# Lags of a chunk's inner products: read from a lagged copy, or as offsets in the inputs on chip

## The chip, the cores and the metric

The kernel runs on one core of a Trainium2 chip. A core has a matrix engine (TensorE, PE in the profile; PEld is its weight load), a vector engine (VectorE, DVE), a scalar engine (ScalarE, ACT), GpSimd (POOL) and SyncE (SP), which here only issues transfers. Each engine works through its own queue in order; they meet at semaphores. Matrix products are written to PSUM, everything else lies in SBUF or in HBM. The metric is the time of one execution on the device, in microseconds; a kernel's time is the median of its runs.

## The reference

One inference step of a two-layer encoder for two groups of requests that share the weights: 256 new frames of one stream and 32 further frames of another, 288 positions with 2048 channels in all. Layer 0 is attention (two kinds of heads) with one input and one output projection. Layer 1, which the change touches, is a diagonal complex state-space layer: channels in groups of 16, each with 64 complex states.

```python
u, z = jnp.split(h @ p['w_in_ssm'][isd], 2, axis=-1)
...
bu_re = jnp.einsum('btgc,gpc->btgp', u, bb_re)
bu_im = jnp.einsum('btgc,gpc->btgp', u, bb_im)
...
ac_re, ac_im, x_re, x_im = lax.associative_scan(combine, (a_re, a_im, bu_re, bu_im), axis=1)
...
y = jnp.einsum('btgp,gcp->btgc', x_re, c_re) - jnp.einsum('btgp,gcp->btgc', x_im, c_im)
...
y = y.reshape(B, T, D_SSM) + p['ssm_d'][isd] * u32
g = jax.nn.gelu(y)
glu = g * jax.nn.sigmoid(g @ p['w_glu'][isd] + p['b_glu'][isd])
out = (glu.astype(x.dtype) * jax.nn.silu(z)) @ p['w_out_ssm'][isd]
```

## The kernel before

All weights stream in once, in tiles of 128 x 2048 (w, 1 MB, rows of 8192 bytes), through four staging slots. Each weight tile is split into a high and a low part (hi by ACT, lo by DVE), the activations likewise (ah, al), and each product is three matmuls into one accumulator m: hi x ah, hi x al, lo x ah. This main stream is some 6900 matmuls of 288 or 290 columns on PE.

The work around it, called side work, is a set of Python generators. A planner (`Plan`) keeps a clock for every engine from cost formulas, and `Tasks.step` lets a generator go on when its inputs are due by that clock. So the order of the instructions on each engine is fixed when the program is built, by planned costs; on the chip each queue then runs in that order, whatever is late. A change of a planned cost shifts the side work of its whole stage.

Layer 1 cuts the sequence into blocks of LC = 8 positions, NJ = 36 blocks in all, and stores positions so that index s (place in the block) is the slow one and j (block) the fast one: a row of 288 elements is 8 pieces of 36. The 2048 channels are 16 tiles of 128 (called chunks here, loop variable i, four of them a quarter). For each chunk:

- `builder` (during layer 0) makes three small matrices from the parameters and stores them in HBM: w1 for the state inputs, v2 for the outputs, and kb, which holds for each lag k the 16 x 16 products inside a block. kb comes from the accumulator k_ps.
- `state_in` stores a quarter of the layer's inputs U (in the buffer MX) to HBM (ud), loads it back regrouped into MX[:, 16:20], and multiplies with w1 (accumulator xin_ps) into X.
- `scan` carries the state from block to block on DVE, 32 steps for a quarter.
- `slices` multiplies the states with v2 (y_ps), evicts to Yg and stores to HBM (yd); `gelus` loads it back (yx) and finishes the layer's activation.
- `inside` adds the part of the output that comes from earlier positions of the same block: position s takes kb of lag k times the input at position s - k. In the row of 288, lag k is a shift by 36 k. The accumulator is t_ps; a DVE multiply-add then writes t_ps + D x U over U.

For `inside`, `lags` prepares a copy. ud has rows padded by 108 zeros; UL[n] is loaded from it with four transfers of 32 partitions, each with another lag l = 0 to 3, so that the 128 partitions of UL hold 4 lags x 32 channels, for each of the four groups of 32 channels. Then t_ps needs two matmuls of 128 rows for each group g of 32 output channels: a = 0 for lags 0 to 3 and a = 1 for lags 4 to 7, shifted by 144 columns. There are two UL buffers; one of them is a staging slot of the weights, taken from the moment when layer 1 starts (`taken`) until its states are done.

In the attention layer the lines of cached keys (CK) and values (CV) share one buffer, so a load of CK waits for the product that reads the CV before it (pvs_ps); Ss are the scores against CK.

Of the kernel before, what the change touches and what calls it, by code (L numbers as in the profile page):

```python
# [8 lines left out]
F32 = mybir.dt.float32  # L9
# [14 lines left out]
LC = 8  # L24
# [247 lines left out]
def build(tc, I, O):  # L272
# [8 lines left out]
    with ExitStack() as ctx:  # L281
# [103 lines left out]
        jobs = []  # L385
        st_of = {}
        pos = dict(load=0, run=0)
        st_free, slot_of, taken = list(range(NST)), {}, []
        more = dict(tiles={}, until=0)

        def pump():
# [16 lines left out]

        def st_done(k):
            del st_of[k]  # L410
            if taken and taken[0] is None:
                taken[0] = slot_of[k]
            else:
                st_free.append(slot_of[k])

        quarters = {}
        split = dict(live=0)
# [401 lines left out]
        def builder():  # L819
            bl_load(0)  # L820
            for i in range(KT):
                bl_load(i + 1)
                pt, raw = bl_in.pop(i)
                bb, rc = (raw[:, j].rearrange("p (g r c) -> p g r c", g=4, r=2) for j in range(2))
                plan.last = max(plan.when(plan.written, t) for t in (pt, raw))
                yield "dve"
                V = views(pt)
                bbar(V, bb)
                yield "next dve"
                v2 = bld.tile([128, 2, 4, 9, 16], F32, name="v2")  # L830
                for ri in range(2):
                    tsum(V, v2[:, ri, :, 0:8], bb, 8, *((("apr", 0), ("api", 1), ALU.subtract),
                                                        (("apr", 1), ("api", 0), ALU.add))[ri])
                    if ri == 0:
                        at = plan.last
                        yield "next dve"
                plan.last = at
                for ri in range(2):
                    yield "any"
                    yield from room()  # L840
                    ps = take([128, 4, 128], "w1_ps")
                    for g in range(4):
                        pe.transpose(ps[:, g, :], v2[:, ri, g, 0:8].rearrange("p k c -> p (k c)"), ident)
                    yield "act"
                    W1 = bld.tile([128, 4, 128], F32, tag="W%d" % ri, name="W1")
                    act.copy(W1, ps)
                    act.dma_start(w1_d[i, :, ri], W1)
                    give(ps)
                    plan.last = plan.when(plan.written, v2)
                yield "next dve"  # L850
                for ri in range(2):
                    tsum(V, v2[:, ri], rc, 9, *((("apr", 0), ("api", 1), ALU.subtract),
                                                (("api", 0), ("apr", 1), None))[ri])
                    if ri == 0:
                        yield "next act dve"
                        bp = bld.tile([128, 4, 2, 2, 16], F32, tag="W0", name="bp")
                        for e in range(2):
                            act.activation(bp[:, :, :, e, :], bb, AF.Copy, scale=hmask[:, e:e + 1])
                act.dma_start(v2_d[i], v2.rearrange("p r g k c -> p r (g k c)"))
                plan.last = plan.when(plan.written, v2)  # L860
                yield "any"
                yield from room()
                kps = take([128, 4, 2, 16], "k_ps")
                for g in range(4):
                    for ri in range(2):
                        for l in range(4):
                            mm(kps[32 * l:32 * l + 32, g], bp[:, g, ri].rearrange("p e c -> p (e c)"),
                               v2[:, ri, g, 3 - l:8 - l:4], start=ri == 0, stop=ri == 1)
                yield "act"
                kb = bld.tile([128, 4, 2, 2, 16], F32, tag="W1", name="kb")  # L870
                for e in range(2):
                    act.activation(kb[:, :, :, e, :], kps, AF.Copy, scale=kmask[:, e:e + 1])
                give(kps)
                act.dma_start(kb_d[i], kb.rearrange("p g a e c -> p (g a e c)"))
                plan.last = plan.done(v2.tensor.name)


# [599 lines left out]
        tsc(hbglu, hbglu, 0.5)  # L1477
        sfin = sp1.tile([128, 2, 64, 2], F32, name="sfin")
        sp.dma_start(sfin[:, 1], I["state"])
        PAD = 3 * NJ  # L1480
        ud = dram.tile([KT, 128, PAD + T], F32, name="ud")
        yd = dram.tile([KT, 128, T], F32, name="yd")
        x1d = dram.tile([128, KT, T], F32, name="x1d")
        U = MX
# [102 lines left out]
                act.dma_start(b, w1_d[k])  # L1587
                w1r.append(b)

        UL, ul_free = {}, []  # L1590

        def lags():

            zero = SZ[:, 0:6, :].rearrange("p a t -> p (a t)")
            pool.memset(zero, 0.0)
            sp.dma_start(ud[:, :, 0:PAD].rearrange("n p t -> p n t"), zero.rearrange("p (n t) -> p n t", n=KT))
            while taken[0] is None:
                yield "w any"
            t = wst.tile([128, 2048], F32, tag="w%d" % taken[0], name="UL")
            ul_free.extend((t[:, 0:4 * T], sl.tile([128, 4 * T], F32, name="UL1")))  # L1600
            row = PAD + T
            for n in range(KT):
                while ("ur", n // 4) not in ready or not ul_free:
                    yield "w any"
                UL[n] = ul_free.pop(0).rearrange("p (g t) -> p g t", g=4)
                for l in range(4):
                    sp.dma_start(UL[n][32 * l:32 * l + 32], bass.AP(ud.tensor, ud.offset + 128 * n * row + l * NJ,
                                                                    [[row, 32], [32 * row, 4], [1, T]]))
                ready.add(("ul", n))
                yield "next any"  # L1610

        def state_in():

            while taken[0] is None:
                yield "w"
            w1_ahead(0)
            for i in range(KT):
                if i % 4 == 0:
                    yield from wait(("u", i // 4))
                    sp.dma_start(ud[i:i + 4, :, PAD:].rearrange("n p t -> p n t"), U[:, i:i + 4, :])  # L1620
                    yield "act"
                    ready.add(("ur", i // 4))
                    ug = MX[:, 16:20, :].rearrange("p a (g j) -> p (a g) j", j=NJ)
                    src = ud[i:i + 4, :, PAD:].rearrange("n (g c) (s j) -> s c (n g) j", c=16, s=LC)
                    for s in range(LC):
                        sp.dma_start(ug[16 * s:16 * s + 16], src[7 - s])
                    yield "act"
# [59 lines left out]

        def kb_load(i):
            if i < KT:
                kbs[i] = sl.tile([128, 4, 2, 32], F32, tag="kb%d" % (i % 3), name="kb")  # L1690
                sp.dma_start(kbs[i].rearrange("p g a e -> p (g a e)"), kb_d[i])

        def slices():

# [33 lines left out]
        def inside():  # L1728

            for i in range(3):  # L1730
                kb_load(i)
            for i in range(KT):
                yield from wait(("ul", i))
                kb = kbs.pop(i)
                plan.last = max(plan.when(plan.written, UL[i]), plan.when(plan.written, kb))
                yield "dve"
                yield from room()
                tps = take([128, T], "t_ps")
                for a in range(2):
                    for g in range(4):  # L1740
                        mm(tps[32 * g:32 * g + 32, 4 * a * NJ:T], kb[:, g, a], UL[i][:, g, 0:T - 4 * a * NJ],
                           start=a == 0, stop=a == 1)
                ul_free.append(UL.pop(i).rearrange("p g t -> p (g t)"))
                kb_load(i + 3)
                dve.scalar_tensor_tensor(U[:, i, :], U[:, i, :], dT[:, i:i + 1], tps, op0=ALU.mult, op1=ALU.add)
                give(tps)
                ready.add(("yt", i))
                yield "next dve"
# [92 lines left out]
        early.close()  # L1841
        banks["mod"] = 0.0
        mod_sb[0] = lambda: sl.tile([128, 8, 8, 16], F32, tag="kb", name="modsb").rearrange("p a b c -> p (a b c)")
        taken.append(None)
        sl = tpool(pd, "sl", 1)
        side.add(state_in())
        side.add(lags())
        side.add(slices())
        side.add(inside())
        for ln in range(2):  # L1850
# [2 lines left out]
        run_jobs(l1b, 4)  # L1853
        side.until(lambda: "mod" in banks and ("yt", KT - 1) in ready)
        del banks["mod"]
        st_free.extend((taken[0], NST))
        free = X.rearrange("p a r j -> p (a r j)")
        more.update(tiles={NST: lambda: free[:, 0:2048].rearrange("p (k n) -> p k n", k=4)}, until=len(jobs))
        side.add(act_split("m1", "g", lambda c: [("glu", c)], lambda c: SZ[:, 4 * c:4 * c + 4, :]))
# [157 lines left out]
```

## Time and profile before

| what | value |
| --- | --- |
| median of 3 runs | 1380.06 us |
| runs | 1374.49, 1380.06, 1509.9 us |
| profiled execution | 1372.13 us |
| its span, first to last instruction | 1369.6 us |
| mean granted TensorE clock | 0.96 |
| moved by DMA | 344.90 MB in 125442 packets, mean 252 GB/s |
| UL loads | 64 transfers of 144 KB |
| store of zeros to ud | one transfer of 864 KB |

Every instruction is recorded through a helper at line 116, so groups are told apart by names: `t_ps<-UL,kb` is what writes t_ps and reads UL and kb. "128*32 128x288" is a matmul with 128 rows and 32 columns of weights that streams 288 columns. A matmul in f32 has two records. A row's last figures are the engine's idle time just before the group and what ended it. In a table by stage, clock and DMA share are means over the stretch. The weights' stream of layer 1 begins near 783 us; its input projection ends near 1122 us, and what follows is the GLU and the output projection.

### The profile page before, as it was taken

To read this page: it belongs to the slowest core of one execution; us is meant where nothing else is said; L and a number is where in the kernel's file an instruction comes from. 1 tells how busy PE (TensorE), PEld (TensorE's weight loads), DVE (VectorE), ACT (ScalarE), POOL (GpSimd) and SP (SyncE) were. 2 spreads that over 40 slices of the span, in tenths; PEclk is the share of its full clock that TensorE was granted. 3 is DMA by queue.
4 is the path that set the end of the run, shared out by engine and by line. 5 is a ranking of instruction groups with operands and counts; after the bars stand their busy time and mean duration, and the time that the engine had idled before them with its cause. 6 is when DMAs were issued, how large, how long until landed. Compare 5 with 4: busy or idle time off the path is not lost.

```text
span 1369.6 us, 28062 instructions
## 1 busy us (share of the span) xinstructions
PE 1237.1 (90%) x11098; PEld 1098.7 (80%) x11098; DVE 922.6 (67%) x2210; ACT 593.4 (43%) x1394; POOL 32.6 (2%) x21
## 2 busy tenths in 40 slices
PE   5999899999898999998899997875997998999996
PEld 3788798888787878886789896764986998989895
DVE  4579978788777877884556953745944965455454
ACT  4533233343454454454443743321553484444341
POOL 0006000000000000000000000000000000000000
PEclk9999999999999999999899998987988999999998
DMA  9978676688878878878665697989499366777631
GB/s 360 372 299 321 233 283 252 232 289 327 308 277 292 314 270 305 308 251 337 231 251 182 210 298 201 236 218 222 150 186 254 132 200 243 262 263 264 245 124 70
DMA packets 125442, 344.90 MB, mean 252 GB/s; under 512 B 50784, under 2 KB 75376, under 8 KB 94592
## 3 DMA queue, kind: packets, MB, share of 16 engines
q1 hardware_dynamic: 112640, 313.47, 67.9%
q10 hardware_dynamic: 12672, 29.65, 5.9%
q8 instruction: 87, 1.43, 0.4%
q14 instruction: 43, 0.35, 0.1%
HBM read 307.13 MB, written 35.95 MB: 250 GB/s over the span
## 4 chain that ended last, share of the span: by engine, by line
issue 44%; PE 32%; DVE 11%; DMA 10%; ACT 2%; POOL 0%; ACTq 0%; SPq 0%; DVEq 0%; POOLq 0%
PE m L116 24%; PE mod_ps L116 4%; DMA w<-in_w_in_att 4%; DVE lo L116 2%; DMA w_d<-W 2%; DMA v_d<-v 2%; DVE v L116 2%; DVE MX L116 1%; DVE tmpv L116 1%; ACT hi L116 1%; PE w_ps L116 1%; DVE qkv L116 1%; DVE dtmp L116 1%; DMA Fb<-Fp_d 1%; DVE ssq L116 1%
## 5 line engine op out<-in xcount | busy, mean ns | idle before, releaser
L116 PE MATMUL m<-ah,hi 128*128 128x288 f32 (+1 forms) x2304 | 714.6, 310 | 13.3 <-ACT hi L116 4.8
L116 PE MATMUL m<-ah,lo 128*128 128x288 f32 (+1 forms) x2304 | 689.8, 299 | 4.3 <-DVE lo L116 4.3
L116 PE MATMUL m<-al,hi 128*128 128x288 f32 (+1 forms) x2304 | 690.7, 300 | 0.4 <-DVE al L116 0.4
L116 PEld LDWEIGHTS m<-ah,hi 128*128 128x128 f32 x2304 | 443.0, 192 | 69.7 <-issue 32.3
L116 DVE TENSOR_TENSOR lo<-w,hi 128x512 fp32r<-128x512 f32 x552 | 368.4, 686 | 169.0 <-ACT hi L116 164.5
L116 ACT CAST hi<-w 128x512 fp32r<-128x512 f32 x552 | 322.0, 617 | 325.0 <-PE m L116 203.3
L116 PEld LDWEIGHTS m<-ah,lo 128*128 128x128 f32 x2304 | 443.2, 192 | 6.2 <-DVE lo L116 6.1
L116 PEld LDWEIGHTS m<-al,hi 128*128 128x128 f32 x2304 | 443.6, 193 | 1.0 <-DVE al L116 0.8
L116 PE MATMUL mod_ps<-w,cs 128*32 128x512 f32 x744 | 97.6, 619 | 12.6 <-DVE ssq L116 12.6
L116 DVE SCALAR_TENSOR_TENSOR qkv<-m,qkv 128x288 f32<-128x288 f32 x168 | 73.0, 452 | 25.9 <-PE m L116 25.7
L116 DVE TENSOR_TENSOR X<-X,t 128x32 f32<-128x32 f32 (+1 forms) x256 | 58.3, 228 | 8.2
L116 DVE TENSOR_TENSOR v<-pt,raw 128x512 f32<-128x512 f32 (+1 forms) x64 | 46.0, 718 | 13.5 <-DMA v_d<-v 13.4
L116 DVE SCALAR_TENSOR_TENSOR MX<-MX,c_dT,t_ps 128x288 f32<-128x288 f32 x16 | 8.2, 512 | 68.5 <-PE t_ps L116 68.5
L116 PE MATMUL t_ps<-UL,kb 128*32 128x288 f32 (+1 forms) x256 | 18.8, 420 | 38.4 <-DMA UL<-ud 38.4
L116 DVE SCALAR_TENSOR_TENSOR MX<-m,gate,MX 128x256 f32<-128x256 f32 x96 | 30.8, 363 | 32.2 <-PE m L116 32.1
L116 PEld LDWEIGHTS mod_ps<-w,cs 128*32 128x32 f32 x744 | 17.2, 110 | 38.0 <-issue 22.2
L116 DVE TENSOR_TENSOR tmpv<-pt,raw 128x512 f32<-128x512 f32 (+1 forms) x64 | 45.9, 718 | 0.0
L116 PEld LDWEIGHTS t_ps<-UL,kb 128*32 128x32 f32 x256 | 8.4, 124 | 46.1 <-issue 42.7
L116 PE MATMUL y_ps<-Xm,v 128*128 128x74 f32 x256 | 34.7, 294 | 10.4 <-DMA v<-v_d 5.3
L116 PEld LDWEIGHTS y_ps<-Xm,v 128*128 128x128 f32 x256 | 33.4, 210 | 11.4 <-ACT Xm L116 6.0
L116 ACT ACTIVATE yx<-MX 128x288 f32<-128x288 f32 (+1 forms) x38 | 18.8, 495 | 50.7 <-DVE MX L116 50.2
L116 DVE TENSOR_TENSOR v<-v,tmpv 128x512 f32<-128x512 f32 (+1 forms) x48 | 34.3, 714 | 1.7
(226 smaller groups left out, 910.6 us busy)
## 6 DMA issues: line engine op xcount, KB each, us to landing
w<-in_w_mod SPq DMA_DIRECT2D x93, 1024.0 KB, 6.2
w<-in_w_in_att SPq DMA_DIRECT2D x40, 1024.0 KB, 7.5
w<-in_w_in_ssm SPq DMA_DIRECT2D x32, 1024.0 KB, 6.7
w<-in_w_wide SPq DMA_DIRECT2D x24, 1024.0 KB, 10.1
w<-in_w_out_att SPq DMA_DIRECT2D x16, 1024.0 KB, 7.0
w<-in_w_glu SPq DMA_DIRECT2D x14, 1024.0 KB, 6.8
w<-in_w_out_ssm SPq DMA_DIRECT2D x12, 1024.0 KB, 5.2
v_d<-v ACTq DMA_DIRECT2D x16, 576.0 KB, 8.3
```

Of the source, the lines that this page charges most:

```text
L116: return f(*a, **k)
```

## The change

The lagged copy and everything that served it is removed: `lags`, the padding of ud, the store of zeros, the slot `taken`. `inside` reads the inputs U where they lie on chip. Partitions 32 g to 32 g + 31 of U hold the 32 channels of group g; a matmul takes those 32 rows and writes the 32 rows of t_ps of the same group, for one lag k, with the row of U cut by 36 k columns. So a chunk has 8 lags x 4 groups = 32 matmuls of 32 x 32 instead of 8 of 128 x 32, and streams 288, 252, ..., 36 columns. `builder` lays kb out to fit: partitions hold (group, channel), the free axis holds the lag, and k_ps takes 8 matmuls of 128 columns for a chunk instead of 32 of 32 columns. kb's size, its two evictions on ACT and its store stay. `inside` of a quarter waits for the store of ud ("ur") instead of the lagged loads ("ul").

```diff
-            if taken and taken[0] is None:
-                taken[0] = slot_of[k]
-            else:
-                st_free.append(slot_of[k])
+            st_free.append(slot_of[k])
...
-                kps = take([128, 4, 2, 16], "k_ps")
-                for g in range(4):
-                    for ri in range(2):
-                        for l in range(4):
-                            mm(kps[32 * l:32 * l + 32, g], bp[:, g, ri].rearrange("p e c -> p (e c)"),
-                               v2[:, ri, g, 3 - l:8 - l:4], start=ri == 0, stop=ri == 1)
+                kps = take([128, 8, 16], "k_ps")
+                for ri in range(2):
+                    for g in range(4):
+                        mm(kps[32 * g:32 * g + 32], bp[:, g, ri].rearrange("p e c -> p (e c)"),
+                           v2[:, ri, g, 0:8], start=ri == 0, stop=ri == 1)
...
-        PAD = 3 * NJ
-        ud = dram.tile([KT, 128, PAD + T], F32, name="ud")
+        ud = dram.tile([KT, 128, T], F32, name="ud")
...
-        def lags():
-
-            zero = SZ[:, 0:6, :].rearrange("p a t -> p (a t)")
-            pool.memset(zero, 0.0)
-            sp.dma_start(ud[:, :, 0:PAD].rearrange("n p t -> p n t"), zero.rearrange("p (n t) -> p n t", n=KT))
...
-            t = wst.tile([128, 2048], F32, tag="w%d" % taken[0], name="UL")
-            ul_free.extend((t[:, 0:4 * T], sl.tile([128, 4 * T], F32, name="UL1")))
-            row = PAD + T
-            for n in range(KT):
-                while ("ur", n // 4) not in ready or not ul_free:
-                    yield "w any"
-                UL[n] = ul_free.pop(0).rearrange("p (g t) -> p g t", g=4)
-                for l in range(4):
-                    sp.dma_start(UL[n][32 * l:32 * l + 32], bass.AP(ud.tensor, ud.offset + 128 * n * row + l * NJ,
-                                                                    [[row, 32], [32 * row, 4], [1, T]]))
...
-                yield from wait(("ul", i))
+                yield from wait(("ur", i // 4))
...
-                for a in range(2):
-                    for g in range(4):
-                        mm(tps[32 * g:32 * g + 32, 4 * a * NJ:T], kb[:, g, a], UL[i][:, g, 0:T - 4 * a * NJ],
-                           start=a == 0, stop=a == 1)
-                ul_free.append(UL.pop(i).rearrange("p g t -> p (g t)"))
+                for k in range(8):
+                    for g in range(0, 128, 32):
+                        mm(tps[g:g + 32, k * NJ:T], kb[g:g + 32, k], U[g:g + 32, i, 0:T - k * NJ],
+                           start=k == 0, stop=k == 7)
...
-        taken.append(None)
         sl = tpool(pd, "sl", 1)
         side.add(state_in())
-        side.add(lags())
         side.add(slices())
         side.add(inside())
```

On PE, the products of the first chunk in the middle of the main stream (m): before,

```order
L116 MATMUL t_ps<-UL,kb 32x288 x4
L116 MATMUL t_ps<-UL,kb 32x144 x4
L116 MATMUL m<-ah,hi 128x290
L116 MATMUL m<-al,hi 128x290
L116 MATMUL m<-ah,lo 128x290
```

and now:

```order
L116 MATMUL t_ps<-MX,kb 32x288 x4
L116 MATMUL t_ps<-MX,kb 32x252 x4
L116 MATMUL t_ps<-MX,kb 32x216 x4
L116 MATMUL t_ps<-MX,kb 32x180 x4
L116 MATMUL t_ps<-MX,kb 32x144 x4
L116 MATMUL t_ps<-MX,kb 32x108 x4
L116 MATMUL t_ps<-MX,kb 32x72 x4
L116 MATMUL t_ps<-MX,kb 32x36 x4
L116 MATMUL m<-ah,hi 128x290
L116 MATMUL m<-al,hi 128x290
L116 MATMUL m<-ah,lo 128x290
```

Two rows of four matmuls became eight. The first of them stands 60 m earlier than the first xin_ps before, and the first two chunks' t_ps now stand ahead of the first xin_ps, which before stood ahead of all t_ps and is itself 36 m earlier now. At the other end, the last y_ps stands 300 m ahead of the end of the input projection, and 36 before.

On SP, the transfers of the first quarter (ud is the store of U, MX<-ud the regrouped load, x8 the eight positions of a block): before,

```order
L116 DMA ud<-MX 128x4x288
L116 DMA w<-in_w_in_ssm 128x2048
L116 DMA MX<-ud 16x32x36 x8
L116 DMA UL<-ud 32x4x288 x4
L116 DMA UL_9942<-ud 32x4x288 x4
L116 DMA w<-in_w_in_ssm 128x2048 x2
L116 DMA kb<-kb_d 128x256
L116 DMA UL<-ud 32x4x288 x4
L116 DMA kb<-kb_d 128x256
```

and now:

```order
L116 DMA ud<-MX 128x4x288
L116 DMA w<-in_w_in_ssm 128x2048
L116 DMA MX<-ud 16x32x36 x8
L116 DMA kb<-kb_d 128x256
L116 DMA w<-in_w_in_ssm 128x2048
L116 DMA kb<-kb_d 128x256 x3
```

The rows of UL are gone, and nothing that stood ahead of MX<-ud moved.

On SP in the attention layer, around the load of the last cached keys, before:

```order
L116 DMA MX<-in_xP 128x1152
L116 DMA w<-in_w_out_att 128x2048
L116 DMA w<-in_w_mod 128x2048
L116 DMA MX<-in_xP 128x1152
L116 DMA CK<-in_kdT 128x4x512
L116 DMA bi<-in_biasS 128x544
```

and now:

```order
L116 DMA pt<-par_d 128x84
L116 DMA raw<-in_b 128x128
L116 DMA raw<-in_c 128x128
L116 DMA CK<-in_kdT 128x4x512
L116 DMA w<-in_w_in_att 128x2048
L116 DMA MX<-in_xP 128x1152
```

The load moved forward, from behind the third and fourth load of the layer's residual input (MX<-in_xP) to ahead of the first. On PE, 126 m now stand between the pvs_ps that frees its buffer and the Ss that reads it; before it was 36. Nothing in the diff names this: it follows from the planned cost of k_ps.

More of the change, by code (lines that the diff above doesn't have):

```diff
@@ L387, in build @@
         pos = dict(load=0, run=0)
-        st_free, slot_of, taken = list(range(NST)), {}, []
+        st_free, slot_of = list(range(NST)), {}
         more = dict(tiles={}, until=0)
@@ L862, in builder @@
                 yield from room()
-                kps = take([128, 4, 2, 16], "k_ps")
-                for g in range(4):
-                    for ri in range(2):
-                        for l in range(4):
-                            mm(kps[32 * l:32 * l + 32, g], bp[:, g, ri].rearrange("p e c -> p (e c)"),
-                               v2[:, ri, g, 3 - l:8 - l:4], start=ri == 0, stop=ri == 1)
+                kps = take([128, 8, 16], "k_ps")
[3 more added lines that the diff above has]
+                           v2[:, ri, g, 0:8], start=ri == 0, stop=ri == 1)
                 yield "act"
-                kb = bld.tile([128, 4, 2, 2, 16], F32, tag="W1", name="kb")
+                kb = bld.tile([128, 8, 2, 16], F32, tag="W1", name="kb")
                 for e in range(2):
-                    act.activation(kb[:, :, :, e, :], kps, AF.Copy, scale=kmask[:, e:e + 1])
+                    act.activation(kb[:, :, e, :], kps, AF.Copy, scale=kmask[:, e:e + 1])
                 give(kps)
-                act.dma_start(kb_d[i], kb.rearrange("p g a e c -> p (g a e c)"))
+                act.dma_start(kb_d[i], kb.rearrange("p k e c -> p (k e c)"))
                 plan.last = plan.done(v2.tensor.name)
@@ L1588, in w1_ahead @@
                 w1r.append(b)
-        UL, ul_free = {}, []
-        def lags():
-            zero = SZ[:, 0:6, :].rearrange("p a t -> p (a t)")
-            pool.memset(zero, 0.0)
-            sp.dma_start(ud[:, :, 0:PAD].rearrange("n p t -> p n t"), zero.rearrange("p (n t) -> p n t", n=KT))
-            while taken[0] is None:
-                yield "w any"
-            t = wst.tile([128, 2048], F32, tag="w%d" % taken[0], name="UL")
-            ul_free.extend((t[:, 0:4 * T], sl.tile([128, 4 * T], F32, name="UL1")))
-            row = PAD + T
-            for n in range(KT):
-                while ("ur", n // 4) not in ready or not ul_free:
-                    yield "w any"
-                UL[n] = ul_free.pop(0).rearrange("p (g t) -> p g t", g=4)
-                for l in range(4):
-                    sp.dma_start(UL[n][32 * l:32 * l + 32], bass.AP(ud.tensor, ud.offset + 128 * n * row + l * NJ,
-                                                                    [[row, 32], [32 * row, 4], [1, T]]))
-                ready.add(("ul", n))
-                yield "next any"
         def state_in():
-            while taken[0] is None:
-                yield "w"
             w1_ahead(0)
@@ L1619, in state_in @@
                     yield from wait(("u", i // 4))
-                    sp.dma_start(ud[i:i + 4, :, PAD:].rearrange("n p t -> p n t"), U[:, i:i + 4, :])
+                    sp.dma_start(ud[i:i + 4].rearrange("n p t -> p n t"), U[:, i:i + 4, :])
                     yield "act"
@@ L1623, in state_in @@
                     ug = MX[:, 16:20, :].rearrange("p a (g j) -> p (a g) j", j=NJ)
-                    src = ud[i:i + 4, :, PAD:].rearrange("n (g c) (s j) -> s c (n g) j", c=16, s=LC)
+                    src = ud[i:i + 4].rearrange("n (g c) (s j) -> s c (n g) j", c=16, s=LC)
                     for s in range(LC):
@@ L1689, in kb_load @@
             if i < KT:
-                kbs[i] = sl.tile([128, 4, 2, 32], F32, tag="kb%d" % (i % 3), name="kb")
-                sp.dma_start(kbs[i].rearrange("p g a e -> p (g a e)"), kb_d[i])
+                kbs[i] = sl.tile([128, 8, 32], F32, tag="kb%d" % (i % 3), name="kb")
+                sp.dma_start(kbs[i].rearrange("p k e -> p (k e)"), kb_d[i])
         def slices():
@@ L1732, in inside @@
             for i in range(KT):
-                yield from wait(("ul", i))
+                yield from wait(("ur", i // 4))
                 kb = kbs.pop(i)
-                plan.last = max(plan.when(plan.written, UL[i]), plan.when(plan.written, kb))
+                plan.last = max(plan.when(plan.written, U[:, i, :]), plan.when(plan.written, kb))
                 yield "dve"
@@ L1855, in build @@
         del banks["mod"]
-        st_free.extend((taken[0], NST))
+        st_free.append(NST)
         free = X.rearrange("p a r j -> p (a r j)")
```

## The prediction

> **What bounds the kernel now.** I read the page first (engines, then the chain of waits), then cut the span into stages, then asked in the one stage that the change rewrites who waits for whom.
>
> ```profile
> span 1369.6 us, 28062 instructions
> PE 1237.1 (90%) x11098; PEld 1098.7 (80%) x11098; DVE 922.6 (67%) x2210; ACT 593.4 (43%) x1394; POOL 32.6 (2%) x21
> issue 44%; PE 32%; DVE 11%; DMA 10%; ACT 2%; POOL 0%; ACTq 0%; SPq 0%; DVEq 0%; POOLq 0%
> L116 PE MATMUL t_ps<-UL,kb 128*32 128x288 f32 (+1 forms) x256 | 18.8, 420 | 38.4 <-DMA UL<-ud 38.4
> ```
>
> PE carries the kernel, so what counts is PE's idle time and PE's own work. The last row holds both sides of this change: the in-chunk products (t_ps) cost PE 18.8 us, and PE stood 38.4 us in front of them for the copy UL that the change removes. The table by stage shows where that is (columns: length, then PE, PEld, DVE, ACT, POOL busy with counts, granted clock, DMA share, GB/s).
>
> ```profile
> 640.00:662.00 22.00, 11.42 (x78) 8.79 (x77) 7.02 (x14) 6.63 (x19) 0.70 (x1) 0.69 0.50 172
> 815.00:1062.00 247.00, 191.56 (x1830) 175.04 (x1830) 137.32 (x461) 90.28 (x243) 0.00 (x0) 0.89 0.84 209
> 1062.00:1140.00 78.00, 73.91 (x559) 73.15 (x558) 59.42 (x154) 47.11 (x113) 0.00 (x0) 1.00 0.57 188
> 1140.00:1152.00 12.00, 7.99 (x38) 7.44 (x37) 7.33 (x13) 5.31 (x10) 0.00 (x0) 0.72 0.51 178
> ```
>
> From 815 to 1062 us PE is idle for 55 of 247 us, the DMA engines are 0.84 busy, and the mean granted clock is 0.89. The waits of that stage, PE's alone (us in total, times, longest):
>
> ```profile
> PE t_ps L116 <- DMA UL<-ud: 38.4, 9, 13.5
> PE y_ps L116 <- DMA v<-v_d: 5.3, 1, 5.3
> PE xin_ps L116 <- DMA UL<-ud: 3.6, 2, 2.0
> PE xin_ps L116 <- DMA MX<-ud: 2.4, 1, 2.4
> PE xin_ps L116 <- DMA SZ<-w_d: 2.1, 1, 2.1
> ```
>
> These are waits in PE's queue: the main product's matmuls (m) behind a late t_ps have their data and stand all the same. After a long one PE also runs slowly for some microseconds, as the timeline shows around one of them and the table by stage for the three longest:
>
> ```profile
> 841.68 1.67 PE L116 MATMUL t_ps<-UL,kb 128*32 128x288 f32 x16 [8.57 <-DMA UL<-ud]
> 922.90 1.67 PE L116 MATMUL t_ps<-UL,kb 128*32 128x288 f32 x16 [7.21 <-DMA UL<-ud]
> 924.91 0.44 PE L116 MATMUL m<-al,hi 128*128 128x290 f32 x1
> 925.15 0.44 PE L116 MATMUL m<-ah,lo 128*128 128x290 f32 x1
> ...
> 927.37 0.30 PE L116 MATMUL m<-al,hi 128*128 128x290 f32 x1
> 927.51 0.30 PE L116 MATMUL m<-ah,lo 128*128 128x290 f32 x1
> ...
> 952.62 1.67 PE L116 MATMUL t_ps<-UL,kb 128*32 128x288 f32 x16 [13.54 <-DMA UL<-ud]
> 836.00:848.00 12.00, 6.32 (x46) 4.40 (x47) 2.90 (x10) 2.62 (x7) 0.00 (x0) 0.57 0.62 132
> 918.00:927.00 9.00, 4.10 (x54) 3.03 (x54) 2.20 (x8) 0.00 (x0) 0.00 (x0) 0.62 1.04 294
> 942.00:958.00 16.00, 5.38 (x38) 4.30 (x42) 4.55 (x21) 0.85 (x3) 0.00 (x0) 0.57 0.99 239
> ```
>
> Matmuls start 0.24 us apart just after the wait and 0.14 us apart later. Read as time at half clock, the three rows hold 2 x (0.43 x 12 + 0.38 x 9 + 0.43 x 16) = 31 us; the waits take 5.7 + 4.9 + 10.6 = 21 us of them, so some 10 us of work ran at half speed and lost 5 us.
>
> **The change, part by part.** More streaming in t_ps. A chunk's products were 2 x 4 matmuls of 288 and 144 columns; now they are 8 x 4 of 288, 252 down to 36 columns. Each of the four 32-column groups streams 1296 columns in place of 432, 864 more. The rate, and whether groups run side by side, come from these rows (mean ns is the second number behind the bar):
>
> ```profile
> L116 PE MATMUL Ss<-CK,qkv 128*32 128x512 f32 x16 | 2.1, 604 | 0.0
> L116 PE MATMUL pvs_ps<-CV,PTs 128*32 128x128 f32 x128 | 4.3, 275 | 0.0
> 400.99 0.42 PE L116 MATMUL pvs_ps<-VS,PTs 32*32 32x128 f32 x8
> 500.08 0.93 PE L116 MATMUL Sd<-qkv,MX 64*128 64x128 f32 x8
> ```
>
> 512 against 128 columns is 329 ns for 384 columns: 0.857 ns a column. Each matmul in f32 stands in the trace twice (x8 for four), so it streams twice. In the third row four matmuls of 32 rows x 32 columns, 8 records of 110 ns, take 0.42 us instead of 0.88: column groups overlap. In the fourth, two row halves of 64, writing two different accumulators, take 0.93 us where one after the other needs 2 x 2 x (128 + 256) x 0.857 = 1.32 us plus the 0.17 us fill (275 less 110): row groups overlap too. The changed t_ps pairs row group g with column group g, and no row shows four such tiles writing one accumulator. If they overlap, a chunk gains 864 x 2 x 0.857 = 1.48 us, 24 us for 16. If they follow one another, it gains (4 x 1296 - 432) x 2 x 0.857 = 8.1 us, 130 us for 16. I take 24, the rows being nearest to that, and keep 130.
>
> The Trainium skill ("TensorEngine Tiling (Array Packing)", Restrictions and Gotchas, PSUM pressure) says that different row tiles cannot access the same PSUM bank at the same time; here all four write one t_ps. By that sentence the sum would take 130 instead of 24. The trace's overlapping row halves wrote different accumulators, so it neither bears the sentence out nor refutes it.
>
> The copy goes. UL needs no more loads: 64 transfers of 32 partitions vanish from SP's queue, and the inputs are on chip once the state path asks for them. The 38 us of waits end, and with them the 5 us at half clock. What is late next is xin_ps, which needs the regrouped inputs (MX from ud):
>
> ```profile
> 802.99 1.17 SPq L116 DMA_DIRECT2D ud<-MX  x1
> 811.33 5.51 SPq L116 DMA_DIRECT2D MX<-ud  x8
> 816.88 4.86 SPq L116 DMA_DIRECT2D UL<-ud  x8
> UL<-ud SPq DMA_DIRECT2D x64, 144.0 KB, 6.7
> ```
>
> (The last row lists the DMA issues: count, size, median us to landing.) The loads MX from ud stand ahead of UL's, so losing UL doesn't advance the first group. In the new order t_ps stands ahead of the first xin_ps: the order has that xin_ps 36 m earlier (5 us at 0.14) and behind two new t_ps of about 2.7 us each (18.8 / 16 + 1.48). It comes at the same moment, and I leave the 8.1 us of xin_ps waits (the rows above) as they are: 0, at most -8.
>
> Relief for other loads. UL's 64 x 144 KB are 9.4 MB of the 52 MB that the stage moves (247 us at 209 GB/s). The wait of y_ps for v (5.3 us, v's load queued between UL's) should go, with half-clock work behind it: -8, from 0 to -17 (the wait, and half of the 23 us at half clock that the stage has besides the 31, since 2 x 0.11 x 247 = 54).
>
> The end of the state path moves forward. In the order, the last y_ps stood 36 m ahead of the end of the input projection; now 300 do. What PE met then was this (the waits from 1062 to 1152, and from 640 to 662 for the next point):
>
> ```profile
> PE m L116 <- ACT ah L116: 3.6, 1, 3.6
> PE m L116 <- DVE lo L116: 2.7, 2, 1.4
> ...
> PE Ss L116 <- DMA CK<-in_kdT: 10.6, 1, 10.6
> ```
>
> The 3.6 us for the split activations and the half clock behind (0.28 x 12 = 3.4 us) go: -7.
>
> The kernel builder. k_ps goes from 32 matmuls of 32 columns to 8 of 128 a chunk, the same columns in sum; one group took 0.76 us:
>
> ```profile
> 281.36 0.76 PE L116 MATMUL k_ps<-v,bp 128*32 128x32 f32 x64
> ```
>
> Eight at 128 columns are four passes of 110 ns and the 0.17 us fill, 0.61 us: -0.15 x 16 = -2. ACT's two evictions and the store keep their sizes. The shorter plan shifts the whole attention stage, though. Between the matmuls that free the buffer of the last cached keys (CK) and the Ss that reads them now stand 126 m, before 36, so the 10.6 us wait should go, and 1.5 us of half clock with it (2 x 0.31 x 22 = 13.6 us, less 10.6, halved). Other lanes move as well, in both directions: I take -8, between -12 and +5.
>
> New waits. With PE no longer idle, the scan on DVE has to keep pace.
>
> ```profile
> L116 DVE TENSOR_TENSOR X<-X,t 128x32 f32<-128x32 f32 (+1 forms) x256 | 58.3, 228 | 8.2
> 960.00:980.00 20.00, 20.00 (x156) 19.83 (x155) 18.56 (x72) 12.79 (x30) 0.00 (x0) 1.00 0.30 94
> ```
>
> In this stretch a scan fills DVE (18.56 of 20) while PE doesn't stop; in the last scan PE lost 2.7 us to lo. Four scans at 2.7, of which some are paid already: +8, from 0 to +25 (a scan of some 35 us standing out by a sixth each time). DVE's multiply-add behind t_ps also waits for the store of ud, as it did, and the m queued behind have split weights in stock: 0. The slot of weights that UL held returns; PE shows no wait for w in the stage, so 0.
>
> The sum: +24 - 38 - 5 - 8 - 7 - 2 - 8 + 8 = -36 us. The profiled execution took 1372.1 us, which gives 1336. The median of the runs is 8 us above it and the fastest 2 above; I put the changed kernel 4 above, 1340 us.
>
> **The rivals.**
> The tiles follow one another (slower). Place: the 32 matmuls of each t_ps. Price: 130 instead of 24, so 1340 + 106 = 1446 us. For it: no row has this form. Against it: rows and columns each overlap alone. It decides once a chunk's t_ps costs over (24 + 36) / 16 = 3.8 us more than now. By the sentence of the Trainium skill above it is so. Chance 0.12.
>
> The wait moves (within 2%). PE stops at xin_ps, y_ps or lo instead, since the path from input projection to scan and the small loads are unchanged. For it: xin_ps already waits 8 us behind the same chain. Against it: t_ps alone has 38 of the 55 us, and the scan row shows PE running. The new waits then stand at +25 and the relief for loads at 0: 1340 + 17 + 8 = 1365 us. Chance 0.27.
>
> The change fails to remove the copy: excluded, no UL stands in the new order.
>
> **How the numbers follow.** The forecast (1313 to 1352) has 0.58, the moved wait (1352 to 1380) 0.27, the serial tiles 0.12, something else 0.03. 2% is about what a measurement of this kernel can tell from no change; from 1380 that is below 1352. The 0.03 is shared out evenly. Faster: 0.59. Same: 0.28. Slower: 0.13. The range of 1313 to 1380 reaches from the sum with xin_ps, the loads and the keys at their best ends (-8, -9 and -4 more) and new waits at 2 instead of 8, to the moved wait with attention at +5 instead of -8 (1378) and a little to spare, and leaves the serial tiles out.
>
> **What the profile after would show.** t_ps should be 512 matmuls and twice the records, busy about 18.8 + 24 = 43 us in all; about 145 means serial tiles. No UL or ud<-SZ. PE's idle time from 815 on should fall by 45 or more, with the clock near 1; if it is found again under xin_ps, y_ps or lo, the wait has moved. Ss should no longer wait for CK. The forecast is wrong if t_ps is above 80 us or if PE's idle in the stage stays above 35.

## The result and the profile after

| | before | after |
| --- | --- | --- |
| median, 4 runs each | 1377.28 us | 1338.01 us |
| profiled execution | 1372.13 us | 1335.96 us |
| its span | 1369.6 us | 1334.2 us |
| mean granted TensorE clock | 0.96 | 0.974 |

The ratio after to before is 0.974, with a 95% interval of 0.969 to 0.979: the change makes the kernel faster. The ratio compares fast runs alone and leaves out the run of before that took 1509.9 us, so it isn't the quotient of the two medians. The profiled execution after is 36.2 us shorter than the one before.

The page of the changed kernel, first the span, the engines and the chain by engine, then the groups that answer to the rows shown of before:

```profile
span 1334.2 us, 27951 instructions
PE 1248.5 (94%) x11098; PEld 1107.4 (83%) x11098; DVE 922.8 (69%) x2210; ACT 593.8 (45%) x1394; POOL 31.1 (2%) x20
issue 43%; PE 31%; DVE 12%; DMA 10%; ACT 3%; POOL 0%; ACTq 0%; SPq 0%; DVEq 0%; POOLq 0%
L116 PE MATMUL y_ps<-Xm,v 128*128 128x74 f32 x256 | 34.3, 292 | 13.0 <-ACT Xm L116 12.8
L116 PE MATMUL t_ps<-MX,kb 32*32 32x288 f32 (+7 forms) x1024 | 40.1, 306 | 2.8 <-DMA kb<-kb_d 2.8
```

t_ps costs 40.1 us instead of 18.8, and the 38.4 us in front of it are 2.8. PE is busier by 11.4 us, and the span is 35.4 us shorter, so 46.8 us of idle time went. To see where, cut the span at the same piece of work in both traces. The main stream is 6912 matmuls m, the same in both; the bounds are the starts of its numbers 1350, 3900, 4110, 5376 and 5664. Table by stage of the kernel before: attention layer, input projection with the state space, start of the GLU (columns as in the prediction).

```profile
260.09:781.05 520.96, 488.66 (x4802) 424.67 (x4800) 389.26 (x827) 248.57 (x633) 9.67 (x13) 0.97 0.78 276
809.37:1121.70 312.33, 252.79 (x2292) 235.52 (x2291) 188.05 (x598) 128.29 (x336) 0.00 (x0) 0.91 0.77 200
1121.70:1169.56 47.86, 43.85 (x306) 41.29 (x305) 28.46 (x48) 23.36 (x47) 0.00 (x0) 0.93 0.72 247
```

The same three stages of the changed kernel:

```profile
260.26:771.31 511.05, 484.56 (x4032) 417.11 (x4030) 387.77 (x821) 246.54 (x630) 8.13 (x12) 0.98 0.79 281
799.90:1093.15 293.25, 270.30 (x3061) 253.68 (x3059) 192.94 (x605) 131.89 (x338) 0.00 (x0) 0.95 0.66 182
1093.15:1133.86 40.71, 40.71 (x306) 38.70 (x305) 24.31 (x42) 21.07 (x43) 0.00 (x0) 1.00 0.71 257
```

The stages lose 9.9, 19.1 and 7.2 us; nothing more changes to the end. In the input projection PE works 17.5 us longer (t_ps 21.3 longer, the rest 3.8 shorter at a granted clock of 0.95 instead of 0.91) and stands 23.0 us instead of 59.5. In the GLU's start it no longer stands at all. What still stands in the changed kernel from 800 to 1150 us, PE's waits (us in total, times, longest):

```profile
PE y_ps L116 <- ACT Xm L116: 12.8, 3, 8.1
PE xin_ps L116 <- DMA yd<-Yg: 3.4, 1, 3.4
PE t_ps L116 <- DMA kb<-kb_d: 2.8, 1, 2.8
PE xin_ps L116 <- DMA MX<-ud: 1.4, 1, 1.4
PE xin_ps L116 <- DMA kb<-kb_d: 1.3, 1, 1.3
PE xin_ps L116 <- issue: 1.1, 1, 1.1
```

The wait for v and those for UL are gone, and y_ps waits 12.8 us for the scan, where it waited 5.1 before (Xm is ACT's copy of the states). Rows of PE and DVE from its timeline (start, duration; in brackets the idle time before and what ended it):

```profile
915.52 4.08 PE L116 MATMUL t_ps<-MX,kb 32*32 32x288 f32 x64 [2.75 <-DMA kb<-kb_d]
...
919.66 0.52 DVE L116 SCALAR_TENSOR_TENSOR MX<-MX,c_dT,t_ps 128x288 f32<-128x288 f32 x1 [14.33 <-PE t_ps L116]
...
940.01 2.20 PE L116 MATMUL y_ps<-Xm,v 128*128 128x74 f32 x9 [3.16 <-ACT Xm L116]
...
986.76 1.51 DVE L116 TENSOR_TENSOR MX<-MX,yx 128x576 f32<-128x576 f32 x2 [7.80 <-DMA yx<-yd]
...
993.30 3.69 PE L116 MATMUL y_ps<-Xm,v 128*128 128x74 f32 x16 [8.12 <-ACT Xm L116]
```

DVE stood 14.3 us with its multiply-add at the head of its queue, and 7.8 us with a product that needs the reloaded yx; the scan's steps stood behind both, and PE got the scan's result 7 to 20 us later, after waits of 3.2 and 8.1 us. That the one made the other is read from the order of DVE's queue; no run tests it alone.

### The profile page after: what moved, and what is told of

Its sections match the earlier page's. It is cut to its first block, busy times and chain, and to the rows that moved or that the text cites. A ratio compares the mean times of both kernels' runs of the same rounds, so it can differ in the third digit from the quotient of the medians.

```text
span 1334.2 us, 27951 instructions
## 1 busy us (share of the span) xinstructions
PE 1248.5 (94%) x11098; PEld 1107.4 (83%) x11098; DVE 922.8 (69%) x2210; ACT 593.8 (45%) x1394; POOL 31.1 (2%) x20
## 4 chain that ended last, share of the span: by engine, by line
issue 43%; PE 31%; DVE 12%; DMA 10%; ACT 3%; POOL 0%; ACTq 0%; SPq 0%; DVEq 0%; POOLq 0%
PE m L116 24%; DMA w<-in_w_in_att 4%; PE mod_ps L116 4%; DMA v_d<-v 3%; DVE lo L116 3%; DVE v L116 2%; DVE MX L116 1%; DMA w_d<-W 1%; DVE tmpv L116 1%; ACT hi L116 1%; DVE qkv L116 1%; DVE dtmp L116 1%; DVE ssq L116 1%; DMA CK<-in_kdT 1%; DVE al L116 1%
## 5 line engine op out<-in xcount | busy, mean ns | idle before, releaser
L116 DVE TENSOR_TENSOR v<-pt,raw 128x512 f32<-128x512 f32 (+1 forms) x64 | 46.0, 719 | 22.1 <-DMA v_d<-v 18.8
L116 PE MATMUL y_ps<-Xm,v 128*128 128x74 f32 x256 | 34.3, 292 | 13.0 <-ACT Xm L116 12.8
L116 ACT ACTIVATE yx<-MX 128x288 f32<-128x288 f32 (+1 forms) x38 | 18.8, 495 | 56.4 <-DVE MX L116 55.8
L116 PE MATMUL t_ps<-MX,kb 32*32 32x288 f32 (+7 forms) x1024 | 40.1, 306 | 2.8 <-DMA kb<-kb_d 2.8
L116 PEld LDWEIGHTS t_ps<-MX,kb 32*32 32x32 f32 x1024 | 28.7, 107 | 14.3 <-issue 4.4
## 6 DMA issues: line engine op xcount, KB each, us to landing
w<-in_w_wide SPq DMA_DIRECT2D x24, 1024.0 KB, 10.3
```

Source lines behind the costliest of these rows:

```text
L116: return f(*a, **k)
```

## The experiments

Two theories of the gain were set against each other. A: what the change removes is a wait in PE's fixed order, because the planner placed t_ps earlier than UL lands. B: it is the copy itself, its traffic and its queue. A third question was whether the four tiles of a lag overlap, on which the predicted +24 us rested. All kernels below were run beside the kernel before on the same chip; each ratio is to that one (its medians there: 1371.98, 1371.16 and 1370.72 us for the three groups of runs).

**Groups one after the other.** The two loops of t_ps exchanged, so that one group's eight lags follow each other on one row and column group.

```diff
-                for k in range(8):
-                    for g in range(0, 128, 32):
+                for g in range(0, 128, 32):
+                    for k in range(8):
```

> The changed kernel with the two loops of t_ps exchanged: group outside, lag inside, so that eight matmuls of one 32 x 32 tile follow one another. Theory (t_ps is cheap only because four tiles in different row and column groups stream side by side): t_ps rises from 40 us busy to about 140, the kernel from 1338 to about 1440 us. Rival (the engine finds independent tiles in its queue by itself, so order inside a chunk doesn't matter): t_ps stays near 40, 1338 us.

Measured: 1524.4 us, ratio 1.110 (1.104 to 1.117). The same 1024 records are there, yet the kernel is 193 us of span longer than the changed one. The timeline has a run of one chunk, where the changed kernel has 2.4 to 4.1 us:

```profile
815.83 16.43 PE L116 MATMUL t_ps<-MX,kb 32*32 32x288 f32 x64
```

and the table by stage has the first runs of this kernel; PE is busy without a gap in all three rows:

```profile
800.30:804.50 4.20, 4.20 (x32) 2.68 (x32) 0.59 (x1) 0.00 (x0) 0.00 (x0) 1.00 1.04 201
804.70:812.40 7.70, 7.70 (x34) 4.45 (x30) 0.00 (x0) 0.00 (x0) 0.00 (x0) 0.50 0.52 47
815.80:832.00 16.20, 16.20 (x64) 9.28 (x64) 0.00 (x0) 0.00 (x0) 0.00 (x0) 0.50 0.19 65
```

Two effects multiply. Tiles of one group do follow one another: half a chunk (32 records) takes 4.2 us at full clock and a whole one 16.4 at half clock, so at full clock a chunk takes some 8.2 us (estimate: half of 16.4), and not 2.4. Streaming alone explains that: 4 x 1296 columns, twice, at the prediction's 0.857 ns are 8.9 us. And after about 4 us of this the granted clock falls to 0.50, though PE never pauses. At full clock all through, 16 chunks would cost 16 x (8.2 - 2.4) = 93 us more than in the changed kernel, near the forecast of some 100; the clock made it 193.

**Pairs of groups.** Groups 0 and 1 take turns through the lags, then 2 and 3.

```diff
-                for k in range(8):
-                    for g in range(0, 128, 32):
+                for h in range(0, 128, 64):
+                    for k in range(8):
+                        for g in (h, h + 32):
```

> The changed kernel with the inner products issued by pairs of groups: groups 0 and 1 take turns through the eight lags, then groups 2 and 3. Theory A (tiles of different row and column groups run at the same time, tiles of one follow one another): a chunk's run takes two times 2.2 instead of 2.2, so 16 chunks take 35 us more at full clock, about 1373 (1365 to 1385). If the clock falls to half while only two of sixteen tiles of the array stream, as it did with one in the run by whole groups (11 to 14 us a chunk), a chunk takes 6 to 9 us and the kernel 1400 to 1450. Theory B (what costs is the order of the lags, not the overlap): 1340.

Measured: 1355.96 us, ratio 0.989 (0.985 to 0.993), below theory A's 1365 to 1385. A chunk's run in the timeline, here and (second row) in the changed kernel:

```profile
804.11 4.44 PE L116 MATMUL t_ps<-MX,kb 32*32 32x288 f32 x64
801.59 2.40 PE L116 MATMUL t_ps<-MX,kb 32*32 32x288 f32 x64
```

Two at a time take 4.4 us where four at a time take 2.4. So overlap sets the time, as theory A says, and not the order of the lags. From its first to its last start a chunk takes 4.24 us instead of 2.21, so 16 chunks cost 16 x 2.03 = 32.5 us more, and some 2 at half clock; the span shows 22.6. The rest comes off PE's waits: in the input projection PE stands 10.5 us instead of 23.0 (for Xm 7.3 instead of 12.8).

**The copy kept, planned later.** The kernel before, with one number changed in its planner: UL is planned to land 8 us later.

```diff
-                end = p.at["dma"] + 2.0
+                end = p.at["dma"] + 2.0 + dict(UL=8.0).get(out.tensor.name.split("_")[0], 0.0)
```

> The kernel before, with nothing altered but the planned landing of UL's loads, 8 us later in the planner's clock; so t_ps stands later in PE's order. Theory A (the gain came from waits that an order too early for UL's landing made): the 38 us of waits on UL fall below 12, and the time to about 1335 us or less, since t_ps streams a third of the columns. Rival B (the copy itself holds the stage, by 64 transfers on SP's queue and on the DMA engines): the waits come back at xin_ps, y_ps or t_ps, and the time stays within 1360 to 1377 us.

Measured: 1340.78 us, ratio 0.975 (0.971 to 0.979). That is the changed kernel's ratio (0.974), with all 64 copies still made, though some 6 us above the 1335 that theory A gave. Its table by stage, for the same three stages:

```profile
260.22:783.48 523.26, 488.90 (x4803) 424.18 (x4800) 389.50 (x827) 248.44 (x633) 9.69 (x13) 0.98 0.77 275
811.84:1093.13 281.29, 247.28 (x2293) 231.94 (x2291) 189.51 (x601) 127.46 (x332) 0.00 (x0) 0.93 0.85 225
1093.13:1133.84 40.71, 40.71 (x306) 38.70 (x305) 26.44 (x47) 23.34 (x51) 0.00 (x0) 1.00 0.73 270
```

and PE's waits in its layer 1, from 800 to 1150 us:

```profile
PE y_ps L116 <- ACT Xm L116: 18.8, 3, 13.6
PE m L116 <- DVE lo L116: 5.8, 2, 4.0
PE xin_ps L116 <- DMA MX<-ud: 3.7, 1, 3.7
PE y_ps L116 <- DMA v<-v_d: 3.0, 1, 3.0
PE t_ps L116 <- DMA UL<-ud: 1.4, 1, 1.4
```

The wait for UL is 1.4 us instead of 38.4, at a DMA share that has risen from 0.77 to 0.85, and UL's loads land hardly sooner after their issue (a median of 5.8 us, 6.7 before): the transfers were not slow, t_ps stood too early. Theory A holds. In this trace the copy is even 12 us better than the change in this stage (281.3 against 293.3), since PE works 23.0 us less and stands 11.1 us more. That lead isn't steady: the last kernel of this section has the same order in the stage and takes 293.6 there. The changed kernel makes up for it in the attention layer, which is 12.2 us shorter there.

**The copies made, but unread.** The changed kernel with the 64 transfers of UL issued again into a buffer of their own; t_ps doesn't read them. (Shown is the core.)

```diff
+        def copies():
+            for n in range(KT):
+                yield from wait(("ur", n // 4), *[("yt", n - 1)] * (n > 0))
+                t = sl.tile([128, 4 * T], F32, tag="UL", name="UL").rearrange("p (g t) -> p g t", g=4)
+                for l in range(4):
+                    sp.dma_start(t[32 * l:32 * l + 32], bass.AP(ud.tensor, ud.offset + 128 * n * T,
+                                                                [[T, 32], [32 * T, 4], [1, T]]))
```

> The changed kernel with the 64 transfers of UL put back (same sizes and rows of 1152 bytes, no padding, into one buffer that nothing reads). Theory A (the waits were the cost, not the traffic): 1338 to 1350 us, the traffic costing the 8 us that the prediction gave as relief, or less. Rival B (the traffic is the cost): 1360 us or more, with PE waiting over 30 us more than in the changed kernel.

Measured: 1343.63 us, ratio 0.979 (0.974 to 0.984), which overlaps the changed kernel's interval. The span is 6.2 us longer, the input projection 7.7 (300.98 against 293.25). The largest wait of that stage is one for a small load behind the copies:

```profile
PE t_ps L116 <- DMA kb<-kb_d: 9.4, 2, 8.0
```

So traffic and queue are worth some 6 us by the medians, which the noise doesn't tell from nothing; the copies also moved PE's order in the later part of the stage, and the run doesn't separate the two.

**The old attention order.** The changed kernel, where k_ps charges the planner 0.41 us more, so that the attention layer gets the order of before.

```diff
                            v2[:, ri, g, 0:8], start=ri == 0, stop=ri == 1)
+                plan.at["pe"] += 0.41
```

> The changed kernel with 0.41 us added to the planner's clock of PE after each k_ps, which restores the attention layer's order of before; the k_ps matmuls stay the new ones. Theory (9.7 us of the gain lie in the attention layer, some 2 of them from k_ps, the rest from the other order): about 1345 us, with Ss waiting for CK late in the attention layer again. Rival (the shorter k_ps makes it, the order is neutral): 1338 us.

Measured: 1348.39 us, ratio 0.980 (0.976 to 0.984). The attention layer, from the same product on, takes 522.37 us:

```profile
259.19:781.56 522.37, 486.62 (x4033) 419.60 (x4031) 387.90 (x822) 247.08 (x630) 8.13 (x12) 0.98 0.76 275
```

Before it was 520.96, in the changed kernel 511.05. The traces of the other kernels agree: the five with the layer's order of before take 521.0 to 524.2 us there, the six with the changed kernel's order 508.7 to 514.1. So the layer's 10 us came with another order that the cheaper k_ps brought about by its planned cost, not with k_ps, whose own busy time falls by 2 us (256 records of 273 ns against 1024 of 196 that overlapped).

**Keys planned later, other landings later, and the two on the copy.** Ss still waits 10.1 us for CK in the changed kernel. The same line of the planner, with CK 8 us later; with CK 8, yx 6 and kb 6; and, on the kernel before, UL 8, CK 8 and yx 6:

```diff
+                end = p.at["dma"] + 2.0 + dict(CK=8.0).get(out.tensor.name.split("_")[0], 0.0)
...
+                end = p.at["dma"] + 2.0 + dict(CK=8.0, yx=6.0, kb=6.0).get(out.tensor.name.split("_")[0], 0.0)
...
+                end = p.at["dma"] + 2.0 + dict(UL=8.0, CK=8.0, yx=6.0).get(out.tensor.name.split("_")[0], 0.0)
```

> The changed kernel with one number of its planner other: CK's transfer is planned to land 8 us later. Theory A (an order that comes before its transfer): the 10.1 us in which Ss waits for CK in the attention layer come from Ss standing too early in PE's row, and the main stream's products, which are independent, fill them once Ss stands later. The wait shrinks under 2 us, start of product 3900 of m falls by 7 to 12 us, the later stages keep their times, and the kernel takes about 1328 (1324 to 1333). Theory B (CK's transfer follows its order): CK is issued later as well, or Ss's followers are what the layer's end waits for; the wait stays near 10 us or another takes its place, and the time stays at 1335 to 1342.

> The changed kernel with three landings planned later: CK by 8, yx and kb by 6 us each. Theory A: besides the 10 us of CK, the waits of the input projection that begin at kb and at yx (t_ps for kb 2.8, y_ps for Xm 12.8, of which 8.1 at 985 go back to DVE's wait for yx) shrink to a third, so that the stage loses another 6 to 12 us and the kernel takes about 1320 (1315 to 1328). Theory B: the four quarters hang together in one chain (inputs, t_ps, multiply-add, scan, y_ps, yd, inputs of the next quarter); placing t_ps later delays y_ps and the yd that the next quarter reads, a wait of xin_ps takes the place, and the time is within 4 us of the run with CK alone.

> The kernel before, copy UL kept, with three landings planned later: UL and CK by 8, yx by 6 us. It tells what the change itself is worth once both orders have room. t_ps is the cheaper one here (19 us against 40). Theory A: with UL's wait gone (1340.8 measured on this chip with UL alone) and the 11 us of CK gone too, 1330 (1325 to 1335); with yx's wait thinner 1322 to 1328. So on equal terms the copy costs nothing and the gain of the change was the order. Theory B (the copies' traffic and their queue place set a floor): no better than 1336.

Measured: 1339.11 us (0.977, 0.973 to 0.981), 1334.92 (0.974, 0.970 to 0.978) and 1336.02 (0.975, 0.970 to 0.980). None differs from the changed kernel. A wait for CK stayed in all three (9.2, 9.1 and 10.3 us). In the first two it moved from the load that Ss waited for at 472 to the last one, which now has 72 m between its pvs_ps and its Ss. In the third, PE's order in the attention layer is still that of before, so the later landing of CK changed nothing there, and that run doesn't test theory A for CK. In the first:

```profile
PE Ss L116 <- DMA CK<-in_kdT: 9.2, 1, 9.2
```

In the second, the wait for Xm fell, as theory A has it, and others grew (PE's waits from 795 to 1130 us):

```profile
PE y_ps L116 <- ACT Xm L116: 7.9, 4, 3.0
PE t_ps L116 <- DMA kb<-kb_d: 4.7, 1, 4.7
PE xin_ps L116 <- DMA MX<-ud: 4.3, 2, 3.3
```

Its input projection takes 291.48 us; four kernels that have the changed kernel's order there take 288.9 to 296.7, so no gain is seen. The times fit theory B (the second run lies 4.2 us below the first, where B had at most 4). Its reason, that the quarters hang together in one chain and a later t_ps delays what the next quarter reads, fits the waits that grew, but no run shows it by itself.

**Keys on another queue.** In the changed kernel CK's late load looks like this, SP's queue and PE:

```profile
453.92 1.08 PE L116 MATMUL pvs_ps<-CV,PTs 128*32 128x128 f32 x32
...
458.73 0.33 SPq L116 DMA_DIRECT2D pt<-par_d  x1
...
464.28 0.38 SPq L116 DMA_DIRECT2D Fb<-Fp_d  x1
472.42 0.33 SPq L116 DMA_DIRECT2D w<-in_w_mod  x1
472.84 0.38 SPq L116 DMA_DIRECT2D Fb<-Fp_d  x1
473.28 0.42 SPq L116 DMA_DIRECT2D CK<-in_kdT  x1
...
482.11 1.93 PE L116 MATMUL Ss<-CK,MX 64*32 64x512 f32 x8 [10.13 <-DMA CK<-in_kdT]
```

The product that reads CV, and so frees the buffer, ends at 455; SP stands from 464.7 to 472.4 in front of a load of w, and CK's transfer is queued behind it. So CK's transfers were given to POOL, whose queue is nearly empty; TensorE's order through the layer stays as it was. A second kernel adds yx and kb planned 6 us later, and a third is the copy with UL planned 8 us later and CK on POOL.

```diff
-                sp.dma_start(ck, I["k%sT" % kd][4 * b:4 * b + 4].rearrange("h d t -> d h t"))
+                pool.dma_start(ck, I["k%sT" % kd][4 * b:4 * b + 4].rearrange("h d t -> d h t"))
```

> The changed kernel with CK's four transfers issued by POOL instead of SP; TensorE's order through the attention layer stays what it was. In the changed kernel CV's last reader starts at 454.9 and CK, which shares CV's buffer, is issued at 473.3, 18 us later, and lands at 482.1. Theory A (SP's queue): the buffer is free at 455 and the issue stands behind SP's waits for lo and mod_ps; from POOL it goes at once, lands near 465, and the 10.1 us wait of Ss at 472 is gone: product 3900 of m 9 to 11 us earlier, the rest unchanged, about 1328 (1323 to 1334). Theory B (the buffer itself, or the transfer): the issue waits for something else at 473, or the transfer takes 18 us when it starts earlier among others; the wait stays over 5 us and the time at 1334 to 1342.

> The same with yx and kb planned to land 6 us later as well, as in the run with three later landings, which took 6 us off the input projection. Theory A: both gains add: 10 of the attention layer and 6 of the input projection, about 1322 (1316 to 1330). Theory B of the run before: 1330 to 1337.

> The kernel before, copy UL kept, UL planned to land 8 us later and CK issued by POOL: no on-chip lags at all. Theory A: UL's wait gone as in the run with UL alone (1340.8) and the 11 us wait of Ss for CK gone too: about 1331 (1325 to 1338), the same as the changed kernel with CK by POOL within 6 us, so the change itself is worth nothing once both orders are mended. Rival: the change is worth more than its order, and this one stays 8 us or more above that one.

Measured: 1332.79 us (0.973, 0.970 to 0.976), 1332.08 (0.972, 0.969 to 0.975) and 1345.45 (0.980, 0.975 to 0.986). In the first, POOL issues CK at 458.11, 0.3 us behind the product that frees the buffer, it lands at 472.28, 5 us before its Ss, and no wait for CK is left in the trace; so the cause was SP's queue. But the layer takes 511.86 us, not 501. PE's waits in the attention layer of that kernel, from 260 to 772 us, led by:

```profile
PE S L116 <- DVE zs L116: 4.0, 1, 4.0
PE w_ps L116 <- issue: 3.6, 1, 3.6
PE w_ps L116 <- DVE MX L116: 3.0, 1, 3.0
PE w_ps L116 <- ACT orow L116: 2.5, 1, 2.5
```

None of these four is that long in the changed kernel. Theory A had the cause, and its range holds the median (1332.79), but not for its reason: nothing was gained in the layer. Of the 10.1 us of wait, 7.9 came back as smaller waits (PE stands 24.3 us in the layer instead of 26.5), and PE works 3.0 us more. The second kernel's gains didn't add either; its time is theory B's. What sets this layer's length, with DMA 0.79 busy and DVE 0.76, stays open. The third kernel's Ss still waits 6.0 us and its y_ps 8.1 for v; its median stays 12.7 us above the first kernel's, as its rival had it, though the two intervals touch. But of the 16 us between the two spans (1346.5 and 1330.5) 11.6 lie in the attention layer (523.46 against 511.86), where the third kernel still has the order of before, so the run doesn't set the copy against the change on equal terms. With UL alone, or UL, CK and yx planned later, the copy was as fast as the change.

## Why the prediction was right, point by point

| step | predicted | measured |
| --- | --- | --- |
| t_ps streams more | +24 us | +21.3 (18.8 to 40.1) |
| waits for UL at t_ps | -38 | -38.4 |
| half clock behind them, relief for other loads | -5 - 8 | -5.3 (v) and -3.8 of PE's other work |
| new waits in the stage | +8 | Xm +7.7, kb +4.1, yd +3.4; xin_ps for UL, MX, SZ -6.7: +8.5 in sum |
| the stage in sum | -19 | -19.1 |
| GLU's start | -7 | -7.2 |
| attention layer: keys and k_ps | -8 - 2 | -9.9 |
| sum | -36 | -36.2 |

(The predicted sum of the stage is 24 - 38 - 5 - 8 + 8. The measured rows give -17.7; the other 1.4 us lie in waits not listed. The sum met to a fraction of a microsecond is luck in part: t_ps came 2.7 us cheaper than its term, and half clock and relief together 3.9 smaller than theirs.)

- **The tiles overlap.** The step rested on rows in which only rows or only columns overlapped. A chunk's run from its first to its last start is 2.21 us; the estimate by one group's 1296 columns, twice, at 0.857 ns was 2.22. The pairs (4.24) and the single groups (16.2 at half clock, half of it, 8.1, as the estimate at full) show that this is overlap. By the sentence of the Trainium skill ("TensorEngine Tiling (Array Packing)", Restrictions and Gotchas) that different row tiles cannot access the same PSUM bank at the same time, the changed kernel should have taken the time of the single groups; in this case, where each row group writes its own 32 partitions, the trace doesn't agree.
- **The wait for UL ended** without reappearing in its size. The rival of the moved wait was half right: PE now waits for the scan, with 12.8 us, inside the range of 0 to 25 given for it. That the same waits end with the copy kept (38.4 to 1.4 us, at 1340.8) shows what the prediction hadn't asked: they were due to the planned landing of UL, and the change was one way out of several.
- **The keys: the step failed in its mechanism.** "The 10.6 us wait should go": the last load of CK, with 126 m ahead of its Ss, did lose its wait, but the load before it took on a wait of 10.1 us at 472, because the shorter plan put 72 m between pvs_ps and Ss there, where 342 had stood, and SP issued the load 18 us after its buffer was free. The layer's gain of the predicted size came from the reordered rest: PE works 4.1 us less in it (488.66 to 484.56, some 2 of them k_ps) and stands 5.8 less, mainly at w_ps. The run with the old order has none of it; the run without any wait for CK gains nothing further. It was the size that came true, not the reason.
- **The threshold for idle time** in the stage ("fall by 45 or more") was too strict: 59.5 to 23.0 is 36.6, and from the stage's start to the kernel's end it is 40.9 (76.9 to 36.0). The prediction's own terms give no more than 35 for the stage (38 for UL and 5 for v, less 8 of new waits). So the threshold didn't follow from its sum, and the sum held.

## What to carry to other kernels

When an engine stands for a transfer in a queue that was ordered by planned times, first give the plan a later landing: here, for UL, one number was worth as much as removing the transfer. It doesn't always help: for CK the same number moved the wait to another load or changed nothing. Small matmuls of 32 x 32 were cheap here only while tiles of different row and column groups took turns (2.4 us a chunk with four, 4.4 with two, some 8 to 16 with one); put the loop over groups innermost. And a wait removed pays only up to the next one: of 10.1 us taken from the attention layer nothing reached its end, and of the 32.5 us added by pairs about two thirds did.

## What the runs showed of the hardware that was not expected

A PE that never pauses can fall to half clock and stay there. With one 32 x 32 tile at a time the granted clock went to 0.50 after about 4 us and stayed so through a run of 16.2 us (rows above). In the run with pairs, behind a wait of 3.2 us, a run of t_ps and the full-size m behind it had half clock for 15 us without a pause:

```profile
932.00:940.20 8.20, 8.20 (x64) 5.52 (x64) 0.00 (x0) 0.00 (x0) 0.00 (x0) 0.51 0.61 211
940.30:943.50 3.20, 3.20 (x16) 2.92 (x15) 3.07 (x8) 0.69 (x2) 0.00 (x0) 0.50 0.41 92
943.50:947.00 3.50, 3.50 (x40) 3.43 (x40) 3.33 (x11) 2.77 (x6) 0.00 (x0) 0.50 0.48 137
```

Four tiles at a time had it back in 4.4 us, in the run with unread copies, behind a wait of 8 us:

```profile
923.70:928.10 4.40, 4.38 (x65) 2.94 (x65) 0.00 (x0) 0.00 (x0) 0.00 (x0) 0.52 1.00 323
928.10:932.00 3.90, 3.90 (x58) 3.69 (x52) 3.54 (x12) 1.08 (x3) 0.00 (x0) 1.00 0.65 122
```

The Trainium skill ("TensorE: Matmul & The Clock Gate", What's actually happening) has the gate follow how busy the PE has been recently, with half rate when idle and full rate after about 3.4 us of work. The last two rows agree; the others don't, if busy means only that PE has work. The single tiles suggest that it counts how much of the array works, but the m that stayed at half clock speak against so simple a reading, and none was tried by itself.
